# A decoder layer on one core: a call of weight sums in another stage, a pair of loads behind another load, one cast in place of two

## The chip, the core and the metric

The kernel runs on one core of a Trainium2 chip. The core has TensorE (PE) for matmuls, VectorE (DVE) and ScalarE (ACT) for elementwise work, GpSimd (POOL) and SyncE (SP). The engines work side by side and meet at semaphores; each takes its own instructions in order. Loads and stores are issued by an engine's instruction stream and are carried out by 16 DMA engines. In this kernel SyncE issues nearly all loads and GpSimd all stores. The metric is the time of one execution in microseconds; the median of several is compared.

## The reference

One layer: a token mixer (a gated short convolution beside a multi-scale causal pooling, then an output projection) and an MLP with squared ReLU, each modulated by a conditioning vector and closed by a residual and a LayerNorm. Tokens 2048, width 1024, hidden width 4096, all in fp32.

```python
mod = (silu(c) @ w_ada + b_ada)[:, None, :]
sh1, sc1, g1, sh2, sc2, g2 = jnp.split(mod, 6, axis=-1)

h = x * (1.0 + sc1) + sh1
z = h @ w_in                                   # 1024 -> 2048
gate_b, gate_c, v_conv, v_pool = jnp.split(z, [512, 1024, 1536], axis=-1)
y_conv = gate_b * _short_conv(gate_c * v_conv, conv_w)
y_pool = _multiscale_pool(v_pool, w_pool, pool_scale)
mix = jnp.concatenate([y_conv, y_pool], axis=-1) @ w_out
x = _layer_norm(ALPHA * x + (1.0 + g1) * mix, ln1_g, ln1_b)

h = x * (1.0 + sc2) + sh2
f = jnp.square(jax.nn.relu(h @ w_mlp_in)) @ w_mlp_out   # 1024 -> 4096 -> 1024
x = _layer_norm(ALPHA * x + (1.0 + g2) * f, ln2_g, ln2_b)
```

## The kernel before

**Tokens and stages.** The 2048 tokens are worked on in two blocks of 1024 (b = 0 and 1). Each block goes through an input projection, the mixing, an output projection (`out_proj`), the up projection of the MLP in eight groups of 512 hidden columns (`up`, g = 0 to 7) and the down projection in 14 steps (`down`, n = 0 to 13).

**One fp32 product is three matmuls.** `split` (L82 to L85) makes of a tile its rounded part (a cast on ScalarE, L84, the "hi" or high part) and the remainder (a subtract on VectorE, L85, the "lo" or low part). `mm3` (L88 to L91) then issues high by high (L89), high by low (L90) and low by high (L91), all into one PSUM bank.

**Seven products for eight.** The large matrix products are done in 2 x 2 blocks with seven block products, which need sums of blocks. Sums of weight blocks are made on the chip and kept in DRAM: `sum_block` loads four blocks of 128 x 512 on SyncE (L961), does four additions or subtractions on VectorE (L96, by `tt`) and issues four stores on GpSimd (L968). It is a generator: its first part issues the loads, its second does the rest. `quarter_sums` takes the next of twelve such pieces of work from a list (source `in_w2q`, goal `wquart`); the results are read in the down projection of the second block alone. `quarter_sums_after` does one whole call in tiles of pool c. Calls stand, before the change, at steps 2, 3, 4, 5, 6, 7 and 10 of the first block's down projection, at two places of the second block's input projection, and in groups 1, 3 and 5 of the second block's up projection (through `aside`, in tiles of pool o).

**Buffers.** Tiles of 128 x 1024 fp32 come from pools with a fixed number of buffers: h 28 (split parts), o 10, c 2, w 6 and r 5 (loaded blocks), and 8 PSUM banks. A load into a buffer waits until the last reader of what stood in it has ended, or until a store from it has landed. Since SyncE issues in order, a load that waits holds all the loads behind it.

**The down projection of the first block.** For step n, `down_operands` loads four blocks of the activations (`usum`, pool r) and four of the weights (`in_w`, pool w), and each is split. The operands of step n + 1 are set up in the code ahead of step n's matmuls; a scheduler then places each instruction into its engine's order. Step n's product is drained from PSUM by `keep` (a copy on ScalarE, L1256) or `add` (VectorE). In steps 5 to 8 `residual` also loads two tiles each of the first sub-layer's result (`nsave`, L1151, pool r), scales them by two broadcast rows (`ag` and `ab`) on VectorE and stores them (`rsave`, L1154).

**The up projection of the second block.** `up(g)` does the seven products in the order 0, 1, 2, 3, 4, 5, 6 and joins and squares the results on VectorE and ScalarE; `save` stores them. The weights of group g + 1 are four blocks, a11 to a22, in pool r, loaded ahead while group g runs. Beside them runs `aside`: in groups 1, 3 and 5 a call of weight sums; for groups 2, 4 and 6 two row broadcasts (L221, 512 KB each, from `in_rows`) and a pair of `nsave` tiles (L1020) into pool o, whose load is started a group early by `next(extra[1])` and whose sums are done in the group itself.

**The output projection of the second block.** `out_proj` walks through seven steps with `matmuls`; after the last matmul of each quarter t a function drains the bank on VectorE (`begin`, `end`, L896 among them). `ops.whole(n)` loads the operands of step n; `whole(6)` has the last of them.

**The opening.** `first_group` begins the input projection of the first block. Its weights come in eight k-blocks; for k = 0 the weight half is cast on ScalarE in two pieces of 128 x 256 (L377 and L386), and each has its remainder on VectorE. The matmuls of k = 0 are 24 at L418, those of k = 1 to 7 are 168.

Of the kernel before, what the change touches and what calls it, by code (L numbers as in the profile page):

```python
# [8 lines left out]
F32 = mybir.dt.float32  # L9
F32R = mybir.dt.float32r  # L10
AF = mybir.ActivationFunctionType
ALU = mybir.AluOpType
# [5 lines left out]
H = 512  # L18
# [11 lines left out]
Q = H // 2  # L30
# [13 lines left out]
def tile_hybrid_layer(ctx: ExitStack, tc: tile.TileContext, opening, xT, x, wada, vec, win0, win,  # L44
                      wins, wpool, wout, wmix, w1, w2, w2q, rows, out):
    nc = tc.nc
# [18 lines left out]
    def t_o(w=T, dt=F32):  # L65
        return mk(big, [P, w], dt, "o", 10)
# [28 lines left out]
    def tt(out_, a, b_, op):  # L95
        done = nc.vector.tensor_tensor(out_, a, b_, op=op)  # L96
        recent[0] = done.ins
        return done
# [258 lines left out]
    def first_group(A):  # L357
        ps = {}

        def loads(k):  # L360
            rows_ = [t_h(F32) for _ in range(2)]
            wr, a = t_r(), t_o()
            for i, r in enumerate(rows_):
                in_turn(r, wada[2 * k + i])
            in_turn(wr[:, :H], win0[k])
            in_turn(a, xT[0, k])
            return rows_, wr, [a[:, hs] for hs in halves]

        done = ada_first()
        wr, a = w0, [w0[:, H:], x0[:, H:]]  # L370
        for k in range(KD):
            wt = t_w()
            hi, lo = t_h(), t_h()
            A.append((hi, lo))
            opened.append(done.ins)
            if k == 0:
                nc.scalar.copy(wt[:, :Q], wr[:, :Q])  # L377
            with tc.issue_after(done.ins):
                if k:
                    nc.scalar.copy(wt[:, :H], wr[:, :H])  # L380
                    tt(wt[:, H:], wr[:, :H], wt[:, :H].bitcast(F32), ALU.subtract)
                for x_, hs in zip(a, halves):
                    high = shifted(hi, x_, k, hs)
                    if k == 0 and hs.start == 0:
                        with tc.issue_after(high.ins):
                            high = nc.scalar.copy(wt[:, Q:H], wr[:, Q:H])  # L386
                        for c in (0, Q):
                            tt(wt[:, H + c : H + c + Q], wr[:, c : c + Q], wt[:, c : c + Q].bitcast(F32), ALU.subtract)
                    if k:
                        nc.scalar.activation(x_, x_, AF.Identity, bias=mod[:, 2 * k + SH1 : 2 * k + SH1 + 1],  # L390
                                             scale=mod[:, 2 * k + SC1 : 2 * k + SC1 + 1])
            if k + 1 < KD:
                rows_, wr_n, a_n = loads(k + 1)
            if k == 0:
                with tc.issue_after(high.ins):
                    for hs, bank in zip(halves, cond_banks):
                        nc.scalar.copy(cond[:, hs], bank)
            elif k + 1 < KD:
                done = dot(2 * k + 2, rows_[0])
            with tc.issue_after(done.ins):  # L400
                for x_, hs in zip(a, halves):
                    if k == 0:
                        sc, sh = (mod[:, 2 * k + i : 2 * k + i + 1] for i in (SC1, SH1))
                        nc.vector.tensor_scalar(x_, x_, sc, sh, op0=ALU.mult, op1=ALU.add)
                    low = tt(lo[:, hs], x_, hi[:, hs].bitcast(F32), ALU.subtract)
            if k + 1 < KD:
                with tc.issue_after(low.ins):
                    for i in range(k > 0, 2):
                        dot(2 * k + 2 + i, rows_[i])
                done = biased(2 * k + 2, 2 * k + 4)  # L410
                wr, a = wr_n, a_n
            for h, hs in enumerate(halves):
                for p in range(3):
                    for m in range(4):
                        if k == 0 and p == 0:
                            ps[m, h] = t_ps()
                        w = (H if p == 1 else 0) + m * P
                        nc.tensor.matmul(ps[m, h], wt[:, w : w + P], A[k][p // 2][:, hs],  # L418
                                         start=k == 0 and p == 0, stop=k == KD - 1 and p == 2)
        return ps  # L420
# [396 lines left out]
    class Operands:  # L817
# [18 lines left out]
        def weights(self, n, g, tile=None):  # L836
            w = ORDER[self.steps[n]][1]
            r = tile or t_r()
            nc.sync.dma_start(r, wosum[g, int(w) - 1] if len(w) == 1 else
                              gout[int(w[1]) - 1, 2 * int(w[0]) - 2 + g])  # L840
            self.w[n, g] = parts(r)


# [19 lines left out]
    def out_proj(b, ops):  # L863
        R, X, Y = [], {}, {}
# [10 lines left out]
        def matmuls(n, banks, new, ks, then):  # L875
            for t in range(4):
                if new and ks[0] == 0:
                    banks[t] = t_ps()
                for k in ks:
                    g, p = k // 2, k % 2  # L880
                    (uh, ul), (wh, wl) = ops.a[n, g], ops.w[n, g]
                    cs = slice(p * H + t * P, p * H + t * P + P)
                    mm3(banks[t], uh[:, cs], ul[:, cs], wh[:, halves[p]], wl[:, halves[p]],
                        new and k == 0, k == 3, not new)
                if then:
                    then(t, banks[t])
# [5 lines left out]
        def end(t, cs, other, scalar=1.0):  # L892
            if t not in mv:
                mv[t] = mk(sm, [P, 8], F32, "mv", 8)
            i = 4 + cs.start // H
            begun[:] = [nc.vector.scalar_tensor_tensor(R[t][:, cs], R[t][:, cs], scalar, other, op0=ALU.mult,  # L896
                                                       op1=ALU.add, accum_out=mv[t][:, i : i + 1]).ins]

        def scale():
            t = late.pop()  # L900
            begun[:] = [nc.vector.tensor_scalar(R[t], R[t], mv[t][:, 0:1], mv[t][:, 6:7], op0=ALU.add,
                                                op1=ALU.mult).ins]
            nc.gpsimd.dma_start(nsave[t], R[t])
# [42 lines left out]
        if b == 0:  # L946
            sum_weights(w1[0], w1sum[0], lambda w: t_w(F32), begun[0], halves[1 : 2])
        ops.whole(6)
        scale()
        matmuls(5, X, False, every, lambda t, ps: end(t + 4, hi_, ps))  # L950
        back(0)
        matmuls(6, X, False, every, last_row)
        scale()
# [3 lines left out]
    def sum_block(src, dst, tiles, p):  # L957
        a, b_ = tiles(T), tiles(T)
        b22, b12, b11, b21 = a[:, :H], a[:, H:], b_[:, :H], b_[:, H:]
        for i, r in ((3, b22), (1, b12), (0, b11), (2, b21)):  # L960
            nc.sync.dma_start(r, src[i][:, p])  # L961
        yield
        tt(b22, b22, b12, ALU.subtract)
        tt(b12, b12, b11, ALU.subtract)
        tt(b11, b22, b11, ALU.add)
        tt(b21, b21, b11, ALU.subtract)
        for i, r in ((2, b22), (0, b12), (1, b11), (3, b21)):
            nc.gpsimd.dma_start(dst[i][:, p], r)  # L968
# [37 lines left out]
    def quarter_sums_after(after):  # L1006
        sums = quarter_sums(t_c)
        next(sums)
        with tc.issue_after(after):
            next(sums, None)  # L1010

    def sum_out(g, tiles):
        sum_blocks([gout[i % 2, i // 2 * 2 + g] for i in range(4)], wosum[g], tiles)
# [1 line left out]
    def aside(g):  # L1015
        if g in REST:
            ag, ab = row(t_o(D), rows[0]), row(t_o(D), rows[1])
            tiles = [t_o(D) for _ in REST[g]]
            for t, r in zip(REST[g], tiles):
                nc.sync.dma_start(r, nsave[t])  # L1020
            yield
            for t, r in zip(REST[g], tiles):
                rest_of(t, r, ag, ab)
        elif g in QUARTER_SUMS:
            sums = quarter_sums(t_o)
            next(sums)
            if g in (3, 5):
                early = t_o()
                nc.sync.dma_start(early, usum[g // 2 - 1, 0])
            yield  # L1030
            next(sums, None)
            if g in (3, 5):
                save_quarters(early, QUARTERED[0], g // 2 - 1)

    def up(g, B, fine):
# [21 lines left out]
        def save(r, i):  # L1057
            if fine and i in QUARTERED and (i or g > 1):
                save_quarters(r, QUARTERED[i], g)
            else:  # L1060
                nc.gpsimd.dma_start(usum[g, i], r)
# [27 lines left out]
        product(4, X, False)  # L1089
        join(c22, X)  # L1090
        save(c22, 3)
        if extra and g:
            next(extra[1], None)
        if g == 0:
            yield
# [12 lines left out]
            nc.scalar.activation(c21[:, ps[p]], X[p], AF.Relu)  # L1108
        nc.scalar.activation(c21, c21, AF.Square)
        save(c21, 1)  # L1110
        s7 = t_o()
        tt(s7, c21, c11, ALU.subtract)
        save(s7, 7)
# [45 lines left out]
    def down(b, F, g2, close):  # L1159
        X, Y = {}, {}  # L1160
# [170 lines left out]
        for n, (i, hf) in enumerate(steps):  # L1331
# [4 lines left out]
                ready = operands(n + 1)  # L1336
            if b == 0 and n < 2:
                ada(G2 + 4 * n, G2 + 4 * n + 4, nc.sync.dma_start, lambda: t_o(D))
            if b == 0 and n in (2, 3, 4, 5, 6, 7, 10):
                quarter_sums_after(ready[1][1])  # L1340
            if b == 0 and 2 <= n < 6:
                sum_x(n - 2, ready[1])
# [235 lines left out]
```

## Time and profile before

| | |
|---|---|
| time, median of 3 runs | 1744.46 us (1742.77 to 1746.51) |
| the profiled execution | 1744.09 us |
| its span | 1742.3 us |
| mean granted clock of TensorE in it | 0.997 |
| instructions in it | 22974 |
| moved by DMA in it | 503.59 MB, mean 289 GB/s |

The span runs from the first to the last instruction recorded; 1.8 us of the execution lie around it. The profile cuts the span into 40 equal slices of 43.6 us. Each digit is the busy share of an engine in tenths, PEclk the granted clock of TensorE in tenths of full speed, DMA the busy share of the DMA engines:

```profile
PE   9999999999999999989999999998999999999998
...
DVE  8897898787777876769786789696877767998897
ACT  5323367554544653536573344774454555776451
POOL 0222220122322001100000100103322221000020
PEclk9999999999999999999999999999999999999999
DMA  9988877678888999998773366557787579998671
```

Of the places named below, the time 753 us (the first block's down projection) lies in the 18th slice, 1100 us (the second block's output projection) in the 26th, and 1214 us (its up projection) in the 28th. In the chain of waits, "issue" is time in which an engine waited for nothing that the profile shows. In a timeline a row is the start, the length, the engine, the line and the operation, and in brackets the idle time ahead of it with what ended it.

### The profile page before, as it was taken

How to read it: one execution, taken by the hardware profiler on the slowest of the kernel's cores; microseconds unless marked ns; L12 is line 12 of the kernel's file. 1: busy time of each engine (PE TensorE's matmuls, PEld its weight loads, DVE VectorE, ACT ScalarE, POOL GpSimd, SP SyncE). 2: the span in 40 equal slices, each digit the busy share in tenths (PEclk: the TensorE clock that was granted, in tenths of full speed). 3: DMA queues.
4: the chain of work that ended last, by engine and by line, in shares of the span. 5: the costliest groups of instructions: out<-in, count | busy, mean ns of one | idle time of the engine just before them, and what ended most of it. 6: DMA issues, size and time to landing. Idle time of an engine off the chain costs nothing.

```text
span 1742.3 us, 22974 instructions
## 1 busy us (share of the span) xinstructions
PE 1720.8 (99%) x8142; PEld 1445.8 (83%) x8142; DVE 1389.7 (80%) x1841; ACT 890.8 (51%) x1207; POOL 271.3 (16%) x483
## 2 busy tenths in 40 slices
PE   9999999999999999989999999998999999999998
PEld 7888888788888888878888888887888888999886
DVE  8897898787777876769786789696877767998897
ACT  5323367554544653536573344774454555776451
POOL 0222220122322001100000100103322221000020
PEclk9999999999999999999999999999999999999999
DMA  9988877678888999998773366557787579998671
GB/s 385 345 313 336 322 274 254 253 274 329 322 326 328 384 403 381 384 340 329 280 265 122 141 223 215 206 192 290 264 314 273 216 250 380 418 365 315 237 259 55
DMA packets 157427, 503.59 MB, mean 289 GB/s; under 512 B 18800, under 2 KB 19584, under 8 KB 157312
## 3 DMA queue, kind: packets, MB, share of 16 engines
q1 hardware_dynamic: 107712, 328.56, 51.8%
q0 software_dynamic: 49600, 173.58, 26.0%
q8 instruction: 63, 1.03, 0.2%
q14 instruction: 52, 0.43, 0.1%
HBM read 344.24 MB, written 157.82 MB: 288 GB/s over the span
## 4 chain that ended last, share of the span: by engine, by line
PE 85%; issue 5%; DMA 5%; DVE 3%; POOL 1%; ACT 0%; SPq 0%; DVEq 0%; POOLq 0%; ACTq 0%
PE ps L89 25%; PE ps L91 25%; PE ps L90 25%; PE ps L1195 7%; PE ps L418 2%; DMA o<-hsave 1%; DVE o L96 1%; DMA usum<-o 1%; PE ps L770 1%; DMA r<-in_w 1%; DVE w L85 1%; DMA o<-in_w2q 0%; DVE h L85 0%; DMA wquart<-c 0%; DMA r<-usum 0%
## 5 line engine op out<-in xcount | busy, mean ns | idle before, releaser
L91 PE MATMUL ps<-h,w 128*128 128x512 f32 x1312 | 510.7, 390 | 4.8 <-DVE w L85 4.8
L89 PE MATMUL ps<-h,w 128*128 128x512 f32 x1312 | 511.0, 390 | 1.3 <-DVE o L96 1.1
L90 PE MATMUL ps<-h,w 128*128 128x512 f32 x1312 | 510.7, 390 | 0.0
L89 PE MATMUL ps<-h,h 128*128 128x512 f32 (+1 forms) x936 | 363.3, 388 | 4.7 <-ACT o L1256 4.7
L91 PE MATMUL ps<-h,h 128*128 128x512 f32 (+1 forms) x936 | 363.4, 388 | 0.0
L90 PE MATMUL ps<-h,h 128*128 128x512 f32 (+1 forms) x936 | 363.1, 388 | 0.0
L84 ACT CAST h<-r 128x1024 fp32r<-128x1024 f32 (+1 forms) x202 | 205.6, 1022 | 258.8 <-PE ps L90 70.9
L85 DVE TENSOR_TENSOR h<-r,h 128x1024 fp32r<-128x1024 f32 (+1 forms) x202 | 238.3, 1184 | 82.9 <-ACT h L84 82.5
L84 ACT CAST w<-r 128x1024 fp32r<-128x1024 f32 x156 | 164.2, 1054 | 256.5 <-PE ps L90 247.5
L91 PEld LDWEIGHTS ps<-h,w 128*128 128x128 f32 x1312 | 246.6, 188 | 56.6 <-DVE w L85 5.2
L89 PEld LDWEIGHTS ps<-h,w 128*128 128x128 f32 x1312 | 246.6, 188 | 53.7 <-DVE o L96 1.1
L90 PEld LDWEIGHTS ps<-h,w 128*128 128x128 f32 x1312 | 246.7, 188 | 51.3 <-DVE h L85 0.3
L85 DVE TENSOR_TENSOR w<-r,w 128x1024 fp32r<-128x1024 f32 x156 | 190.3, 1220 | 81.8 <-ACT w L84 81.1
L89 PEld LDWEIGHTS ps<-h,h 128*128 128x128 f32 x936 | 176.2, 188 | 41.2 <-ACT o L1256 5.1
L91 PEld LDWEIGHTS ps<-h,h 128*128 128x128 f32 x936 | 176.2, 188 | 36.0
L90 PEld LDWEIGHTS ps<-h,h 128*128 128x128 f32 x936 | 176.1, 188 | 35.8
L85 DVE TENSOR_TENSOR h<-w,h 128x1024 fp32r<-128x1024 f32 x130 | 159.4, 1226 | 9.4 <-ACT h L84 9.1
L84 ACT CAST h<-w 128x1024 fp32r<-128x1024 f32 x130 | 136.5, 1050 | 22.5 <-DMA w<-in_w 15.4
L96 DVE TENSOR_TENSOR o<-o,o 128x512 f32<-128x512 f32 (+2 forms) x172 | 127.9, 747 | 6.7 <-DMA o<-hsave 4.5
L96 DVE TENSOR_TENSOR o<-o,ps 128x512 f32<-128x512 f32 (+1 forms) x150 | 96.0, 650 | 42.3 <-PE ps L91 39.7
L1195 PEld LDWEIGHTS ps<-h,h 128*128 128x128 f32 x1008 | 121.1, 192 | 0.1
L1195 PE MATMUL ps<-h,h 128*128 128x256 f32 x1008 | 121.1, 283 | 0.0
(175 smaller groups left out, 1532.7 us busy)
## 6 DMA issues: line engine op xcount, KB each, us to landing
r<-usum SPq DMA_DIRECT2D x88, 512.0 KB, 6.6
usum<-o POOLq DMA_DIRECT2D x64, 512.0 KB, 5.3
w<-w2sum SPq DMA_DIRECT2D x64, 512.0 KB, 6.1
r<-in_w SPq DMA_DIRECT2D x60, 512.0 KB, 6.2
r<-uquart SPq DMA_DIRECT2D x42, 512.0 KB, 5.9
o<-in_w SPq DMA_DIRECT2D x72, 256.0 KB, 6.0
w2sum<-o POOLq DMA_DIRECT2D x64, 256.0 KB, 7.4
usum<-c POOLq DMA_DIRECT2D x26, 512.0 KB, 5.8
```

The lines of the kernel that those rows point to most:

```text
L84: high = nc.scalar.copy(hi, src)
L85: return high.ins, nc.vector.tensor_tensor(lo, src, hi.bitcast(F32), op=ALU.subtract).ins
L89: nc.tensor.matmul(ps, whi, xhi, start=first, stop=False, skip_group_check=goes_on)
L90: nc.tensor.matmul(ps, whi, xlo, start=False, stop=False, skip_group_check=goes_on)
L91: nc.tensor.matmul(ps, wlo, xhi, start=False, stop=last, skip_group_check=goes_on)
L96: done = nc.vector.tensor_tensor(out_, a, b_, op=op)
L418: nc.tensor.matmul(ps[m, h], wt[:, w : w + P], A[k][p // 2][:, hs], start=k == 0 and p == 0, stop=k == KD - 1 and p == 2)
L770: nc.tensor.transpose(ps[:, t * P : t * P + P], R[4 * h + t][:, k * P : k * P + P], ident)
L1195: nc.tensor.matmul(ps, a[:, us], w[:, gs], start=not begun, stop=hf == 1 and g == 3 and a is ul, skip_group_check=True)
```

## The change

Three edits. (1) The call of weight sums at step n = 7 of the first block's down projection is dropped, and one call is put into the second block's output projection: its loads are issued behind the last weight load of `ops.whole(6)`, and its sums come in two pieces behind quarters 2 and 3 of `matmuls(5, ...)`. For that `sum_block` has a second `yield`. The twelve pieces are the same; those behind the dropped call each come one call earlier or in the new place. (2) In `up(1)` the loads of the third group's rows and pair (`aside(2)`) are started behind the last `save` but one, and no longer behind `save(c22, 3)`. (3) In `first_group` the cast for k = 0 is one of 128 x 512, and so is its remainder.

```diff
@@ first_group
             if k == 0:
-                nc.scalar.copy(wt[:, :Q], wr[:, :Q])
+                nc.scalar.copy(wt[:, :H], wr[:, :H])
             with tc.issue_after(done.ins):
                 if k:
                     nc.scalar.copy(wt[:, :H], wr[:, :H])
-                    tt(wt[:, H:], wr[:, :H], wt[:, :H].bitcast(F32), ALU.subtract)
+                tt(wt[:, H:], wr[:, :H], wt[:, :H].bitcast(F32), ALU.subtract)
                 for x_, hs in zip(a, halves):
                     high = shifted(hi, x_, k, hs)
-                    if k == 0 and hs.start == 0:
-                        with tc.issue_after(high.ins):
-                            high = nc.scalar.copy(wt[:, Q:H], wr[:, Q:H])
-                        for c in (0, Q):
-                            tt(wt[:, H + c : H + c + Q], wr[:, c : c + Q], wt[:, c : c + Q].bitcast(F32), ALU.subtract)
@@ Operands.weights
-            nc.sync.dma_start(r, wosum[g, int(w) - 1] if len(w) == 1 else
-                              gout[int(w[1]) - 1, 2 * int(w[0]) - 2 + g])
+            self.loaded = nc.sync.dma_start(r, wosum[g, int(w) - 1] if len(w) == 1 else
+                                            gout[int(w[1]) - 1, 2 * int(w[0]) - 2 + g]).ins
@@ out_proj
         ops.whole(6)
+        if b:
+            sums = quarter_sums(t_c)
+            with tc.issue_after(ops.loaded):
+                next(sums)
         scale()
-        matmuls(5, X, False, every, lambda t, ps: end(t + 4, hi_, ps))
+
+        def last_half(t, ps):
+            end(t + 4, hi_, ps)
+            if b and t > 1:
+                with tc.issue_after(begun[0]):
+                    next(sums, None)
+
+        matmuls(5, X, False, every, last_half)
@@ sum_block
         tt(b12, b12, b11, ALU.subtract)
+        yield
         tt(b11, b22, b11, ALU.add)
@@ quarter_sums_after
         with tc.issue_after(after):
-            next(sums, None)
+            for _ in sums:
+                pass
@@ aside
-            next(sums, None)
+            for _ in sums:
+                pass
@@ up
         save(c22, 3)
-        if extra and g:
+        if extra and g > 1:
             next(extra[1], None)
...
         save(c21, 1)
+        if extra and g == 1:
+            next(extra[1])
@@ down
-            if b == 0 and n in (2, 3, 4, 5, 6, 7, 10):
+            if b == 0 and n in (2, 3, 4, 5, 6, 10):
                 quarter_sums_after(ready[1][1])
```

How instructions move is best seen at two places. A row is the line in the code, the operation, and the tiles it writes and reads with the number that the tile has in its kernel; the numbers differ between the two kernels, since tiles are counted through. In the code after, L961 becomes L967, L1121 becomes L1132, L1123 becomes L1134, L1151 becomes L1162, L514 becomes L509 and L1020 becomes L1028.

**The first block's down projection, around step 7.** SyncE's order before, from the last load for step 7 on; r tiles from `nsave` are the pair for `residual`, c tiles are those of the call of sums:

```order
L1123 DMA w_976_6143<-in_w2 128x1024
L961 DMA c_981_6153<-in_w2q 128x512 x2
L1151 DMA r_983_6167<-nsave_151 128x1024
L961 DMA c_982_6154<-in_w2q 128x512 x2
L1151 DMA r_984_6172<-nsave_151 128x1024
L1121 DMA r_985_6277<-usum_149 128x1024
L1123 DMA w_986_6279<-in_w2 128x1024
L1121 DMA r_991_6289<-usum_149 128x1024
```

SyncE's order after, from the same load on:

```order
L1134 DMA w_976_6141<-in_w2 128x1024
L1162 DMA r_981_6151<-nsave_151 128x1024
L1162 DMA r_982_6156<-nsave_151 128x1024
L1134 DMA w_984_6263<-in_w2 128x1024
L1132 DMA r_983_6261<-usum_149 128x1024
L1134 DMA w_990_6275<-in_w2 128x1024
L1134 DMA w_996_6287<-in_w2 128x1024
L1132 DMA r_989_6273<-usum_149 128x1024
```

The c loads are gone from between the nsave loads, and weight loads now stand ahead of the usum load that has the second place in its step (r_991 before, r_989 after). In both, that usum load takes the buffer of r_969, and the first nsave load that of r_957; the second nsave load waits for the store of r_952 to `rsave`.

VectorE's order at the same place before, from the last operation on step 7's first operands on:

```order
L85 TENSOR_TENSOR h_968_6126<-w_964_6119,h_967_6125 128x1024
L96 TENSOR_TENSOR r_983_6167<-r_983_6167,o_921_5817 128x1024
L96 TENSOR_TENSOR r_983_6167<-r_983_6167,o_922_5819 128x1024
L85 TENSOR_TENSOR h_972_6134<-r_969_6129,h_971_6133 128x1024
L85 TENSOR_TENSOR h_974_6138<-w_970_6131,h_973_6137 128x1024
L96 TENSOR_TENSOR r_984_6172<-r_984_6172,o_921_5817 128x1024
L96 TENSOR_TENSOR r_984_6172<-r_984_6172,o_922_5819 128x1024
L85 TENSOR_TENSOR h_978_6146<-r_975_6141,h_977_6145 128x1024
```

VectorE's order after, from the same operation on:

```order
L85 TENSOR_TENSOR h_968_6124<-w_964_6117,h_967_6123 128x1024
L96 TENSOR_TENSOR r_981_6151<-r_981_6151,o_921_5815 128x1024
L96 TENSOR_TENSOR r_982_6156<-r_982_6156,o_921_5815 128x1024
L96 TENSOR_TENSOR r_981_6151<-r_981_6151,o_922_5817 128x1024
L85 TENSOR_TENSOR h_972_6132<-r_969_6127,h_971_6131 128x1024
L85 TENSOR_TENSOR h_974_6136<-w_970_6129,h_973_6135 128x1024
L96 TENSOR_TENSOR r_982_6156<-r_982_6156,o_922_5817 128x1024
L85 TENSOR_TENSOR h_978_6144<-r_975_6139,h_977_6143 128x1024
```

The multiplication of the second nsave tile (r_984 before, r_982 after) moved from behind the low part of r_969 to ahead of it.

**The second block's up projection, group 1.** SyncE's order before, from the third weight block of group 2 on; o_1568 and o_1569 belong to the call of sums, the next four tiles to `aside(2)`, r_1591 is the fourth weight block:

```order
L514 DMA r_1590_9896<-in_w1 128x1024
L961 DMA o_1568_9744<-in_w2q 128x512 x2
L961 DMA o_1569_9745<-in_w2q 128x512 x2
L221 DMA o_1573_9793<-in_rows 128x1024
L221 DMA o_1574_9795<-in_rows 128x1024
L1020 DMA o_1575_9797<-nsave_151 128x1024
L1020 DMA o_1576_9798<-nsave_151 128x1024
L514 DMA r_1591_9897<-in_w1 128x1024
```

SyncE's order after, from the same block on:

```order
L509 DMA r_1590_9894<-in_w1 128x1024
L967 DMA o_1568_9742<-in_w2q 128x512 x2
L967 DMA o_1569_9743<-in_w2q 128x512 x2
L509 DMA r_1591_9895<-in_w1 128x1024
L221 DMA o_1582_9874<-in_rows 128x1024
L221 DMA o_1583_9876<-in_rows 128x1024
L1028 DMA o_1584_9878<-nsave_151 128x1024
L1028 DMA o_1585_9879<-nsave_151 128x1024
```

The fourth weight block moved from behind the four loads of `aside(2)` to ahead of them.

VectorE's order there before, from the second of the weight sums on; r_1602 is the sum of two weight blocks, ps tiles are banks of the group's products, o_1567 is what `join` adds them to, and w_1593 and w_1598 are low parts for products 0 and 1 of group 2:

```order
L96 TENSOR_TENSOR o_1568_9744<-o_1568_9744,o_1569_9745 128x512
L96 TENSOR_TENSOR o_1567_9741<-o_1567_9741,ps_1500_9354 128x512
L96 TENSOR_TENSOR o_1569_9745<-o_1568_9744,o_1569_9745 128x512
L96 TENSOR_TENSOR o_1569_9745<-o_1569_9745 128x512
L96 TENSOR_TENSOR o_1567_9741<-o_1567_9741,ps_1501_9367 128x512
L85 TENSOR_TENSOR w_1593_9903<-r_1588_9894,w_1592_9902 128x1024
L96 TENSOR_TENSOR o_1561_9706<-o_1561_9706,ps_1565_9715 128x512
L96 TENSOR_TENSOR r_1602_9977<-r_1590_9896,r_1591_9897 128x1024
L96 TENSOR_TENSOR o_1561_9706<-o_1561_9706,ps_1566_9728 128x512
L85 TENSOR_TENSOR w_1598_9936<-r_1589_9895,w_1597_9935 128x1024
```

VectorE's order there after, from the same sum on:

```order
L96 TENSOR_TENSOR o_1568_9742<-o_1568_9742,o_1569_9743 128x512
L96 TENSOR_TENSOR o_1567_9739<-o_1567_9739,ps_1500_9352 128x512
L96 TENSOR_TENSOR o_1569_9743<-o_1568_9742,o_1569_9743 128x512
L96 TENSOR_TENSOR r_1602_9975<-r_1590_9894,r_1591_9895 128x1024
L96 TENSOR_TENSOR o_1569_9743<-o_1569_9743 128x512
L96 TENSOR_TENSOR o_1567_9739<-o_1567_9739,ps_1501_9365 128x512
L85 TENSOR_TENSOR w_1593_9901<-r_1588_9892,w_1592_9900 128x1024
L96 TENSOR_TENSOR r_1590_9894<-r_1588_9892,r_1590_9894 128x1024
L96 TENSOR_TENSOR o_1561_9704<-o_1561_9704,ps_1565_9713 128x512
L96 TENSOR_TENSOR r_1588_9892<-r_1602_9975,r_1588_9892 128x1024
L96 TENSOR_TENSOR o_1561_9704<-o_1561_9704,ps_1566_9726 128x512
L85 TENSOR_TENSOR w_1598_9934<-r_1589_9893,w_1597_9933 128x1024
```

The sum r_1602, which reads the fourth weight block, moved ahead of the add on ps_1501 and of the low part w_1593.

## The prediction

> **What bounds the kernel now.** I read the busy table first, then what TensorE waited for.
>
> ```profile
> PE 1720.8 (99%) x8142; PEld 1445.8 (83%) x8142; DVE 1389.7 (80%) x1841; ACT 890.8 (51%) x1207; POOL 271.3 (16%) x483
> ```
>
> ```profile
> PE ps L91 <- DVE w L85: 4.8, 1, 4.8
> PE ps L89 <- ACT o L1256: 4.7, 1, 4.7
> PE ps L418 <- ACT h L229: 1.2, 2, 0.9
> PE ps L89 <- DVE o L96: 1.1, 2, 0.7
> ```
>
> TensorE is busy for 99% of the span, so work taken from another engine gains nothing by itself: only TensorE's gaps can be won. Two single waits, 4.8 and 4.7 us, are far above the rest. The timeline of TensorE shows where they stand; the rows of 1213.83 and 14.75 are for later.
>
> ```profile
> 14.75 38.39 PE L418 MATMUL ps<-h,w 128*128 128x512 f32 x168 [0.30 <-ACT h L229]
> ...
> 753.17 0.39 PE L91 MATMUL ps<-h,h 128*128 128x512 f32 x1
> 758.22 0.50 PE L89 MATMUL ps<-h,h 128*128 128x512 f32 x1 [4.67 <-ACT o L1256]
> ...
> 1213.83 0.50 PE L89 MATMUL ps<-h,w 128*128 128x512 f32 x1 [0.19 <-ACT c L1045]
> 1214.17 0.40 PE L90 MATMUL ps<-h,w 128*128 128x512 f32 x1
> 1219.34 0.77 PE L91 MATMUL ps<-h,w 128*128 128x512 f32 x1 [4.78 <-DVE w L85]
> ```
>
> Matmuls start 38.39 / 168 = 0.2285 us apart. **Stall B** lies in the first block's down projection and loses 758.22 − 753.17 − 0.23 = 4.82. **Stall C** lies in up group 2 of the second block and loses 1219.34 − 1214.17 − 0.23 = 4.94. Behind each, the table by windows (length, then sum and count for PE, PEld, DVE, ACT and POOL, then the granted clock, the DMA share, GB/s) has a stretch at half clock:
>
> ```profile
> 758.60:762.02 3.42, 3.42 (x10) 2.65 (x9) 2.80 (x3) 3.02 (x5) 1.08 (x2) 0.50 0.99 405
> 1219.40:1222.82 3.42, 3.42 (x8) 2.72 (x9) 3.42 (x5) 0.00 (x0) 0.75 (x1) 0.50 1.03 246
> ```
>
> Each loses another 0.5 × 3.42 = 1.71. So B costs 6.53 and C 6.65; I found no half clock behind the smaller gaps.
>
> **Stall C: the load moved ahead of the row pair.** SyncE's queue issues in order. Before, the fourth weight block of group 2 (r_1591) stands behind two row broadcasts and the nsave pair. The rows: SyncE, the landing of the first row broadcast, the chain of waits, VectorE.
>
> ```profile
> 1183.95 3.58 SPq L221 DMA_DIRECT2D o<-in_rows  x2
> ```
>
> ```profile
> DMA to landing us min/median/max: 11.8/12.0/12.1
> ```
>
> ```profile
> 1191.42 13.35 DMA r<-in_w
> ```
>
> ```profile
> 1183.06 1.22 DVE L85 TENSOR_TENSOR w<-r,w 128x1024 fp32r<-128x1024 f32 x1
> ...
> 1193.68 0.68 DVE L96 TENSOR_TENSOR o<-o,ps 128x512 f32<-128x512 f32 x1
> ...
> 1204.86 1.22 DVE L96 TENSOR_TENSOR r<-r,r 128x1024 f32<-128x1024 f32 x1 [8.76 <-DMA r<-in_w]
> ...
> 1218.07 1.22 DVE L85 TENSOR_TENSOR w<-r,w 128x1024 fp32r<-128x1024 f32 x1
> ```
>
> The block is issued at 1191.42, lands 13.35 later at 1204.77, and VectorE stands 8.76 us at its first use; everything behind it is late, down to the low part at 1218.07 for which TensorE waits in product 2. After, only the four weight-sum loads precede it. Its buffer is free when the subtract of 1183.06 ends (1184.28), so it is issued where the first row broadcast was, and by that row's 11.8 it lands at 1184.0 + 11.8 = 1195.8, nine microseconds earlier.
>
> What is late next? VectorE's order changes too: the sum that needs r_1591 now stands ahead of the add that ran at 1193.68, and that add frees a PSUM bank. Work: sum 1.14 (spacing of such 1.22 us rows), two half-width operations of 0.60: the bank is free at 1195.8 + 2.4 = 1198.2. Products take 24 × 0.2285 = 5.48 us; counted back from product 2 at 1213.83 less the 0.35 lost just before it, product 1 begins at 1208.0, product 0 at 1202.5, product 6 of the group before at 1197.1, and its second half, which takes that bank, at 1199.8. Margin 1.6. From 1198.2 VectorE has nine full-width and two half-width operations up to the low part for product 2: 9 × 1.14 + 2 × 0.60 = 11.5, done at 1209.7 against a need at 1213.5. Margin 3.8. So all of C goes: **−6.65**. What is unknown is the landing: the quick end is 6 us or so (gain the same), the late end the 13.35 of the old row, which gives 1197.7 and a loss of 0.1 us. I take 11.8, the load that stood at this very place. The pair and its rows now land later; their first use on VectorE stands behind the low part for product 2 in its order.
>
> **Stall B: a call of weight sums is taken out.** The chain, SyncE, VectorE, ScalarE in that order:
>
> ```profile
> 736.06 6.82 DMA wquart<-c
> ...
> 750.58 5.96 DMA r<-usum
> ```
>
> ```profile
> 740.76 0.82 SPq L961 DMA_DIRECT2D c<-in_w2q  x2
> 741.68 0.38 SPq L1151 DMA_DIRECT2D r<-nsave  x1
> ```
>
> ```profile
> 733.95 1.22 DVE L85 TENSOR_TENSOR h<-r,h 128x1024 fp32r<-128x1024 f32 x1
> ...
> 746.92 2.48 DVE L96 TENSOR_TENSOR r<-r,o 128x1024 f32<-128x1024 f32 x2 [7.76 <-DMA r<-nsave]
> 749.33 1.22 DVE L85 TENSOR_TENSOR h<-r,h 128x1024 fp32r<-128x1024 f32 x1
> ```
>
> ```profile
> 756.64 1.04 ACT L84 CAST h<-r 128x1024 fp32r<-128x1024 f32 x1 [3.06 <-DMA r<-usum]
> 757.59 0.58 ACT L1256 COPY o<-ps 128x512 f32<-128x512 f32 x1
> ```
>
> The removed call's loads (740.76) waited for buffers whose stores were still under way, and held SyncE; behind them the nsave load (741.68) came late; VectorE waited for it until 746.92, did two operations on it and the low part of 749.33, which frees the buffer of the usum load issued at 750.58. That lands at 756.54; ScalarE casts it, and only then makes the copy of 757.59 that frees TensorE's bank: TensorE goes on 1.68 after the landing.
>
> After, those c loads are gone, but VectorE's order changes with them: both nsave tiles are multiplied ahead of that low part. The second (r_982) needs the buffer that a store has to leave, of which GpSimd's timeline and the tile's landing say:
>
> ```profile
> 733.72 0.54 POOL L1154 DMA_DIRECT2D rsave<-r  x1 [0.59 <-DVE r L96]
> ```
>
> ```profile
> DMA to landing us min/median/max: 7.9/7.9/7.9
> ```
>
> ```profile
> DMA to landing us min/median/max: 5.1/5.1/5.1
> ```
>
> The first nsave load can go when the subtract of 733.95 ends (735.2, instead of 741.68). The second cannot go before 733.72 + 7.9 = 741.6; I take 742.3, as the first load now shares the DMA engines with that store. The nsave row took 5.1 with two c loads beside it (0.52 MB, 1.3 us at the 405 GB/s above); without them 3.9, so it lands at 746.2 instead of 746.8. Three operations later, as before (746.8 to 750.58 is 3.78), the usum load is issued at 750.0; by its old 5.96 it lands at 755.9, and 1.68 later, at 757.6, TensorE goes on. Loss 757.6 − 753.17 − 0.23 = 4.2 instead of 4.82. The head-of-line wait is thus **moved to another store, not removed**. The half clock: both stretches are 3.42 long and begin 0.38 and 0.06 after the restart, as if periods of 3.42 were judged and one with no more than 0.38 of work were called idle. An idle time of 4.0 holds such a period in (4.0 + 0.38 − 3.42) / 3.42 = 28% of positions, so I leave the half clock out. B falls from 6.53 to 4.2: **−2.3**. Bounds: if the second load did not bind (landed by 744), loss 2.0; if the usum load also took 4 us, nothing; on the other side the shared store lands a whole 1.3 us later and the loss with half clock is 7.2, 0.7 more than before.
>
> The Trainium skill, "TensorE: Matmul & The Clock Gate", section "Part 1: The HAM clock gate", gives a free-running window of 3413 ns and half rate after one idle window. The two rows of 3.42 agree; by it alone, with no work allowed in the window, a gap of 4.0 would lose the clock in 17% of positions.
>
> A rule of the skill speaks against this part: "DMA: Bandwidth & Descriptors", section "Queues, rings and completion order", says that a DMA engine takes turns between queues, packet by packet. So a load issued earlier on SyncE's queue slows a store on GpSimd's; by it the gating store would land up to the 1.3 us later, and B would be the 7.2 of the bound. That is part of the first rival.
>
> **The call moved into the output projection.** Four loads, four sums of 0.68 us, four stores. VectorE and GpSimd there:
>
> ```profile
> 1105.60 0.69 DVE L896 SCALAR_TENSOR_TENSOR o<-o,ps 128x512 f32<-128x512 f32 x1 [1.18 <-PE ps L91]
> ...
> 1108.33 0.69 DVE L896 SCALAR_TENSOR_TENSOR o<-o,ps 128x512 f32<-128x512 f32 x1 [2.04 <-PE ps L91]
> ```
>
> ```profile
> 1110.51 0.53 POOL L782 DMA_DIRECT2D hsave<-r  x1 [5.86 <-ACT r L775]
> ```
>
> The loads stand behind the last weights of the projection, over 20 us ahead of the sums. A pair of sums (1.3) fits into the idle 2.04 ahead of 1108.33 and the next pair behind it, and GpSimd is idle for 5.86. I cost it at **0**; the bounds are nothing and 4 × 0.60 = 2.4, if every sum stood on TensorE's path.
>
> **The opening cast.** ScalarE and VectorE:
>
> ```profile
> 7.53 0.41 ACT L377 CAST w<-r 128x256 fp32r<-128x256 f32 x1 [4.86 <-DMA r<-in_opening]
> ...
> 11.72 0.62 ACT L380 CAST w<-r 128x512 fp32r<-128x512 f32 x1 [1.11 <-DMA r<-in_win]
> ```
>
> ```profile
> 11.27 1.22 DVE L207 SCALAR_TENSOR_TENSOR h<-h,o 128x1024 f32<-128x1024 f32 x1
> ```
>
> The first cast becomes 0.21 longer (0.62 against 0.41), and the first matmuls start later by it. But TensorE waits 0.30 at 14.75 for a tile of the second block, which hangs on VectorE's operation of 11.27. VectorE does one subtract of 0.61 in place of two of 0.33 and then the same tiles, and I get 11.28 for that operation. The 0.21 goes out of the later 0.30: **0**, between −0.1 and +0.2.
>
> **The sum** on the profiled run's own 1744.09 (span 1742.3 and 1.8 around it): 1744.09 − 6.65 − 2.3 = 1735.1. The median shown is 1744.46, 0.37 above that run: **1735.5**.
>
> **The rivals.** *B stays whole*: the wait moves to the store and the load behind it, TensorE resumes near 758 and loses the clock. For it: VectorE's new order and the 7.9 of the store. 1744.46 − 6.65 = 1737.8. *Both go*: the second nsave load is quick and the usum load lands by 751.7. Against it: it would take 4 us off a chain of which I can name 0.6. 1744.46 − 6.65 − 6.53 = 1731.3. *The bank in product 6*: r_1591 lands 2.4 past the 1197.4 from which the margin is gone: 1737.9. *C only changes its place*: it lands between 1201.5 and 1204, product 6 stands for 4 to 7 us and half clock follows: 1741 to 1746. *The other side*: the load gains nothing by its new place and lands at 1204.8 as before. Then product 6 stands for 7.4 and loses 1.71 of clock, 9.1 in place of 6.65, and with B whole the kernel is **slower**: 1744.46 + 2.45 = 1746.9. It is worse than before from a landing of 1202.7 on. Against both: the row broadcast at that place landed at 1195.8.
>
> **How the numbers follow.** Forecast 0.50, B whole 0.24, both gone 0.11, product 6 late 0.05, C only moved 0.06, the other side 0.04. The range takes in the first four, with the runs' spread at its ends (1.7 below their median, 2.05 above): 1731.3 − 1.7 = 1729.6 to 1737.9 + 2.0 = 1739.9. A measurement can tell about 0.2% (3.5 us) from no change. Faster by more: the first four, 0.90. Within it: C only moved and half of the other side, 0.08. Slower: the other half, 0.02.
>
> **What would show it.** For C: the in_w load that VectorE's first sum needs is issued near 1184 and lands near 1196, and the wait on the L85 low part with its half clock is gone; a wait of L89 on VectorE's add in product 6 would show the late bank. For B: an nsave load at about 735, one behind the rsave store at about 742, VectorE waiting until about 746, and a TensorE gap near 4 us with full clock behind it. Wrong would be: a gap at the output projection's sums, a longer span up to 53 us, or a gap of 5 us and more at either place.

## The result and the profile after

The changed kernel takes 1736.48 us (median of 6 runs, 1735.78 to 1738.29), against 1745.10 for the kernel before (6 runs, 1742.76 to 1746.51) beside it: a ratio of **0.9955, 95% interval 0.9942 to 0.9967**, faster by 0.45%. The forecast was 1735.5, range 1729.6 to 1739.9. The profiled run of the changed kernel took 1735.78, its span is 1734.0.

What TensorE waited for, in the kernel after (in all, times, longest):

```profile
PE ps L89 <- ACT o L1267: 5.6, 1, 5.6
PE ps L127 <- DVE tmp L122: 1.1, 1, 1.1
PE ps L413 <- ACT h L229: 0.6, 1, 0.6
```

The wait of 4.8 on the low part (stall C) is gone. The wait on the copy (L1267, L1256 before; stall B) is not: 5.6 instead of 4.7. TensorE's timeline after, at the places where the same matmul was shown before:

```profile
752.06 0.39 PE L91 MATMUL ps<-h,h 128*128 128x512 f32 x1
758.02 0.80 PE L89 MATMUL ps<-h,h 128*128 128x512 f32 x1 [5.57 <-ACT o L1267]
...
761.55 0.39 PE L89 MATMUL ps<-h,h 128*128 128x512 f32 x1
...
1212.99 0.39 PE L89 MATMUL ps<-h,w 128*128 128x512 f32 x1
...
1215.26 0.39 PE L90 MATMUL ps<-h,w 128*128 128x512 f32 x1
...
1725.85 0.28 PE L91 MATMUL ps<-h,h 128*128 128x256 f32 x1
```

Its counterparts before that have not been shown yet:

```profile
345.11 0.50 PE L89 MATMUL ps<-h,w 128*128 128x512 f32 x1 [0.67 <-DVE o L96]
...
761.93 0.43 PE L89 MATMUL ps<-h,h 128*128 128x512 f32 x1
...
1222.87 0.39 PE L90 MATMUL ps<-h,w 128*128 128x512 f32 x1
...
1733.49 0.28 PE L91 MATMUL ps<-h,h 128*128 128x256 f32 x1
```

The same matmul in both, after less before, tells where the 8.3 us between the spans were won and lost:

| up to | before | after | difference | won (−) or lost (+) on the way |
|---|---|---|---|---|
| the last matmul ahead of stall B | 753.17 | 752.06 | −1.11 | −1.11 |
| behind B and its half clock | 761.93 | 761.55 | −0.38 | +0.73 |
| the start of product 2 of group 2 | 1213.83 | 1212.99 | −0.84 | −0.46 |
| behind C and its half clock | 1222.87 | 1215.26 | −7.61 | −6.77 |
| the last matmul | 1733.49 | 1725.85 | −7.64 | −0.03 |
| the end of the span | 1742.3 | 1734.0 | −8.3 | −0.66 |

C gave 6.77 and, with the small wait ahead of it, 7.23. B gave nothing and took 0.73 in this pair of profiles. The 1.11 ahead of B are not the change's: small gaps like the one at 345.11, in a stretch where no instruction was changed, are there in one profile and missing in the next. In the ten profiles of this case, all with the same work and order there, gaps above 0.8 us between the starts of two matmuls came four times near 317 and once near 345. The 0.66 at the end lie behind the last matmul.

**Stall C went as worked out.** SyncE and VectorE after:

```profile
1183.73 0.33 SPq L509 DMA_DIRECT2D r<-in_w  x1
```

```profile
1194.62 1.22 DVE L96 TENSOR_TENSOR r<-r,r 128x1024 f32<-128x1024 f32 x1 [2.07 <-DMA r<-in_w]
...
1196.37 0.68 DVE L96 TENSOR_TENSOR o<-o,ps 128x512 f32<-128x512 f32 x1
...
1207.62 1.22 DVE L85 TENSOR_TENSOR w<-r,w 128x1024 fp32r<-128x1024 f32 x1
```

The load is issued at 1183.73 and VectorE uses it at 1194.62 (forecast 1184 and 1195.8). The bank that the new order put at risk is free at 1196.37 + 0.68 = 1197.05 (forecast 1198.2), 2.2 ahead of its need (1212.99 − 2.5 × 5.48 = 1199.3). The low part for product 2 is done at 1208.84 (forecast 1209.7), before the product begins at 1212.99.

**Stall B only moved.** The chain of waits after, from the store on:

```profile
732.94 8.95 DMA rsave<-r
...
741.91 3.74 DMA r<-nsave
...
748.02 1.23 DVE h L85
...
749.27 7.08 DMA r<-usum
...
757.39 0.59 ACT o L1267
```

SyncE's timeline has the two nsave loads as one row from 734.41 to 742.23:

```profile
734.41 7.82 SPq L1162 DMA_DIRECT2D r<-nsave  x2
```

The second of them is issued 0.02 after the rsave store lands (732.94 + 8.95 = 741.89). Before, the chain ran over a wquart store (736.06 + 6.82 = 742.88). VectorE stands for the nsave loads as before, and ScalarE stands at the cast ahead of the copy:

```profile
742.36 1.23 DVE L96 TENSOR_TENSOR r<-r,o 128x1024 f32<-128x1024 f32 x1 [3.96 <-DMA r<-nsave]
745.74 2.36 DVE L96 TENSOR_TENSOR r<-r,o 128x1024 f32<-128x1024 f32 x2 [2.16 <-DMA r<-nsave]
748.02 1.22 DVE L85 TENSOR_TENSOR h<-r,h 128x1024 fp32r<-128x1024 f32 x1
```

```profile
756.44 1.04 ACT L84 CAST h<-r 128x1024 fp32r<-128x1024 f32 x1 [6.24 <-DMA r<-usum]
757.39 0.58 ACT L1267 COPY o<-ps 128x512 f32<-128x512 f32 x1
```

The theory after this, not yet shown here: B is an order, and twice so. On VectorE a multiplication that waits for an nsave load stands ahead of the low part that frees a loading buffer; on ScalarE copies that are ready stand behind a cast that waits for the load into that buffer. The rival is the number of bytes: the DMA engines are 99% busy from 752 to 766 before and 96% after, and if that is a limit, no order helps.

### The profile page after: what moved, and what is told of

The parts are those of the page before. It is cut to its first block, busy times and chain, and to the rows that moved or that the text cites. A ratio compares the mean times of both kernels' runs of the same rounds, so it can differ in the third digit from the quotient of the medians.

```text
span 1734.0 us, 22976 instructions
## 1 busy us (share of the span) xinstructions
PE 1718.8 (99%) x8142; PEld 1446.1 (83%) x8142; DVE 1388.4 (80%) x1840; ACT 890.8 (51%) x1206; POOL 272.1 (16%) x483
## 3 DMA queue, kind: packets, MB, share of 16 engines
q8 instruction: 63, 1.03, 0.2%
## 4 chain that ended last, share of the span: by engine, by line
PE 94%; issue 3%; DMA 1%; DVE 1%; POOL 0%; ACT 0%; SPq 0%; DVEq 0%; POOLq 0%; ACTq 0%
PE ps L89 28%; PE ps L90 28%; PE ps L91 28%; PE ps L1206 7%; PE ps L413 3%; PE ps L765 1%; DMA rsave<-r 1%; DMA r<-usum 0%; DMA r<-in_opening 0%; DMA r<-nsave 0%; POOL wquart L975 0%; DVE o L96 0%; DVE h L85 0%; POOL rsave L1165 0%; POOL xsum L593 0%
```

## The experiments

All times are medians; each ratio is to runs of the kernel before on the same chip (1744.49 for the first four, 1744.11 for the other four).

### The load of group 2's fourth weight block alone (`e_pair`)

The kernel before with this edit:

```diff
         save(c22, 3)
-        if extra and g:
+        if extra and g > 1:
             next(extra[1], None)
...
         save(c21, 1)
+        if extra and g == 1:
+            next(extra[1])
```

> Before with the second edit alone (the fourth weight block of group 2 ahead of the rows and the pair). Theory: stall C hangs on the place of that load alone. The load is issued near 1184 to 1185 and lands near 1196, the gap at product 2 and its half clock are gone, the gap of about 5 us in the first block's down projection stays: 6.7 to 7.3 us faster, about 1738. Rival: C went because of what the other edits moved in time; then a gap of 2 us or more stays in group 2 and the gain is under 4.

1738.70 (6 runs), ratio 0.9969 (0.9957 to 0.9981), which is 5.4 us faster (3.3 to 7.5); the expected 6.7 to 7.3 lie in the interval, above its middle. The only wait of TensorE that is listed from 20 us on:

```profile
PE ps L89 <- ACT o L1258: 5.8, 1, 5.8
```

The other large wait is gone. The gap in the first block's down projection stands. The edit alone takes C away, and the rival falls.

### The call of weight sums alone (`e_call`)

The kernel before with the edits to `Operands.weights`, `out_proj`, `sum_block`, `quarter_sums_after`, `aside` and the list of steps in `down`, as in the diff of the change.

> Before with the first edit alone (one call of weight sums taken from step 7 of the first block's down projection and put into the second block's output projection). Theory: the wait only moves, to the rsave store and the nsave load behind it, and TensorE goes on between 757 and 759 as it did before: no change, within 1.5 us of before, gap of 4 to 6 us at step 8 with half clock, nothing above 0.3 us at the output projection. Rival (the forecast): the stall is about 2.3 shorter and so is the time.

1745.39 (12 runs), ratio 1.0004 (0.9995 to 1.0013). TensorE's waits:

```profile
PE ps L89 <- ACT o L1270: 5.4, 1, 5.4
PE ps L91 <- DVE w L85: 4.8, 1, 4.8
```

No gain shows: the interval leaves at most 0.9 us. The 2.3 of the forecast are ruled out. No gap shows at the output projection. The theory holds: TensorE goes on at 758.59.

### The opening cast alone (`e_open`)

The kernel before with the edit to `first_group`.

> Before with the third edit alone (the opening cast whole). Theory: from the start of the first cast to VectorE's first L207 operation 3.74 us as in both profiles, so no change of the time beyond 0.3 us; the 0.70 by which k = 1 began later in the changed kernel came from the landing of the opening load. Rival: the whole cast itself costs 0.7 us.

1744.35 (12 runs), ratio 1.0000 (0.9992 to 1.0009): nothing, within 1.6 us. That the changed kernel's k = 1 began 0.7 later has its cause in the opening load. ScalarE's first cast in the kernel of `e_pair`, which has not this edit, and in that of `e_copy`, which has it:

```profile
8.29 0.41 ACT L377 CAST w<-r 128x256 fp32r<-128x256 f32 x1 [5.46 <-DMA r<-in_opening]
```

```profile
7.60 0.62 ACT L377 CAST w<-r 128x512 fp32r<-128x512 f32 x1 [4.72 <-DMA r<-in_opening]
```

The late landing came without the edit, the early one with it. From the first cast to VectorE's L207 operation it is 11.27 − 7.53 = 3.74 before and 12.02 − 8.27 = 3.75 after. The wait at B, in a kernel that has the call at step 7 as before, is longer here than the 4.7 of the first profile:

```profile
PE ps L89 <- ACT o L1251: 5.4, 1, 5.4
```

### ScalarE's copies ahead of the casts (`e_copy`)

The changed kernel with:

```diff
         def keep(t, cs, ps):
-            nc.scalar.copy(F[t][:, cs], ps)
+            kept[:] = [nc.scalar.copy(F[t][:, cs], ps).ins]
...
             elif n + 1 < len(steps):
-                ready = operands(n + 1)
+                with tc.issue_after(kept[0]) if b == 0 and n == 8 else nullcontext():
+                    ready = operands(n + 1)
```

> The changed kernel, with ScalarE's casts for step 9 of the first block's down projection ordered behind the four copies that drain step 7. Theory: stall B is an order on ScalarE, copies that are ready standing behind a cast that waits for a load; the load itself is not needed for 20 us. TensorE then has no gap above 1 us at step 8 and no half clock there, and the time is 6 to 7.5 us below the changed kernel, about 1729.5. Rival: the stretch is bound by what the DMA engines can move, so the operands are late anyway and a gap of 3 us or more comes back in steps 8 to 10; time within 3 us of the changed kernel.

1736.20 (6 runs), ratio 0.9955 (0.9942 to 0.9968): no gain over the changed kernel that these intervals, some 2 us to each side, could show. The gap at step 8 is gone; at step 9 TensorE now waits four times, 4.2 us in all:

```profile
777.01 0.50 PE L90 MATMUL ps<-h,h 128*128 128x512 f32 x1 [2.38 <-DVE h L85]
779.28 0.50 PE L90 MATMUL ps<-h,h 128*128 128x512 f32 x1 [0.61 <-DVE h L85]
```

That is the gap which the rival had asked for, but its reason is not there. VectorE, GpSimd and the table by windows:

```profile
764.08 2.48 DVE L96 TENSOR_TENSOR r<-r,o 128x1024 f32<-128x1024 f32 x2 [10.03 <-DMA r<-nsave]
773.46 1.23 DVE L96 TENSOR_TENSOR r<-r,o 128x1024 f32<-128x1024 f32 x1 [6.89 <-DMA r<-nsave]
774.61 1.22 DVE L85 TENSOR_TENSOR h<-r,h 128x1024 fp32r<-128x1024 f32 x1
```

```profile
766.87 0.53 POOL L1165 DMA_DIRECT2D rsave<-r  x1 [14.25 <-DVE r L96]
```

```profile
770.00:777.00 7.00, 4.63 (x21) 3.50 (x19) 3.54 (x4) 0.00 (x0) 0.00 (x0) 1.00 0.28 81
```

The DMA engines are 28% busy while TensorE waits. VectorE stands twice at operations on nsave tiles, for 10.0 and 6.9 us; the second nsave load, issued at 770.12, had to wait for the rsave store of 766.87, which took 3.2. Only behind it come the low parts of step 9, 1.14 us apart; TensorE's waits are two of them apart (779.28 − 777.01 = 2.27). So ScalarE's order was the last link of stall B. That VectorE's pair is the root, which then made the next gap, is a reading of these rows; the next experiment tests it. The theory was right on step 8 and wrong in expecting the time.

### VectorE's pair behind the low parts (`e_rest`)

The changed kernel with:

```diff
-            tt(r, r, ag, ALU.mult)
-            tt(r, r, ab, ALU.add)
+            with tc.issue_after(after[1]):
+                tt(r, r, ag, ALU.mult)
+                tt(r, r, ab, ALU.add)
             nc.gpsimd.dma_start(rsave[t], r)
             if t % 2:
-                yield
+                after = yield
```

> The changed kernel, with VectorE's four operations on each pair of nsave tiles ordered behind the last low part of the step whose operands were set up just before; ScalarE's order is left to itself. Theory: the root of stall B and of the gap at step 9 in the kernel with the copies first is VectorE standing at a multiplication whose nsave load waits for an rsave store. With it behind the low parts the buffer of the gating usum load is free near 739, that load is issued near 743 (SyncE still waits for the store) and lands near 749, before TensorE needs the copy at 752: no gap above 1 us in steps 8 to 10, 6 to 7 us below the changed kernel, about 1730. Rival: SyncE's own wait at the nsave load and the bytes in this stretch hold the usum load anyway: a gap of 3 us or more stays.

1731.95 (6 runs), ratio 0.9921 (0.9908 to 0.9934): by the two ratios 0.34% or 5.9 us below the changed kernel, where 6 to 7 were expected. The wait of 5.57 has become one of 0.90, and one of 0.3 behind it, with no half clock:

```profile
754.48 0.50 PE L89 MATMUL ps<-h,h 128*128 128x512 f32 x1 [0.90 <-ACT o L1268]
```

ScalarE still has the casts of two operand pairs of step 9 ahead of the copies, and they wait for loads, if much shorter. The theory holds, but for this last 1 us. One thing the edit does not separate: it orders VectorE alone, but the loads on SyncE have moved too. A usum load now stands ahead of both nsave loads, the first of which was issued at 734.41 in the changed kernel:

```profile
741.00 0.33 SPq L1132 DMA_DIRECT2D r<-usum  x1
741.42 0.95 SPq L1162 DMA_DIRECT2D r<-nsave  x2
```

So what is shown is the effect of the new order on both engines; how much of it is VectorE's alone is not.

### Both orders (`e_both`)

The edits of `e_copy` and `e_rest` together.

> The changed kernel with both orders: VectorE's pair behind the low parts, and ScalarE's casts for step 9 behind the copies of step 7. Theory: no gap above 1 us in steps 8 to 10, and since one of the two orders is enough at step 8, within 1 us of the kernel with VectorE's order alone, about 1730. Rival: the DMA engines bound the stretch, gaps of 2 us or more come back in steps 9 to 11.

1729.19 (4 runs), ratio **0.9908 (0.9894 to 0.9922)**: by the two ratios 0.47% or 8 us below the changed kernel, in which B costs 7.2 (758.02 − 752.06 − 0.23 = 5.73, and some 1.5 at half clock). No gap is left in the down projection. VectorE's low part of 746.52 now comes ahead of the pair, and ScalarE copies as soon as TensorE lets it:

```profile
746.52 1.23 DVE L85 TENSOR_TENSOR h<-r,h 128x1024 fp32r<-128x1024 f32 x1 [5.16 <-ACT h L84]
747.66 1.22 DVE L85 TENSOR_TENSOR h<-w,h 128x1024 fp32r<-128x1024 f32 x1
748.80 3.49 DVE L96 TENSOR_TENSOR r<-r,o 128x1024 f32<-128x1024 f32 x3
```

```profile
748.65 0.59 ACT L1269 COPY o<-ps 128x512 f32<-128x512 f32 x1 [1.21 <-PE ps L91]
```

It is 2.8 below `e_rest` by the medians where the theory had said within 1; the two intervals overlap, so how much the second order adds to the first stays open.

### Both orders, and the call back at step 7 (`e_both_call7`)

As `e_both`, with:

```diff
-        if b:
-            sums = quarter_sums(t_c)
-            with tc.issue_after(ops.loaded):
-                next(sums)
         scale()
...
-            if b and t > 1:
-                with tc.issue_after(begun[0]):
-                    next(sums, None)
...
-            if b == 0 and n in (2, 3, 4, 5, 6, 10):
+            if b == 0 and n in (2, 3, 4, 5, 6, 7, 10):
```

> As the kernel with both orders, but the call of weight sums stands at step 7 of the first block's down projection again and none in the output projection. Theory: the stall was an order, not the call's bytes or its place, so with the orders right the call costs nothing there: within 1.5 us of the kernel with both orders. Rival: the call's loads and stores (1 MB each way) are what is too much for the stretch: 2 us or more slower, with a gap in steps 8 to 10.

1729.05 (4 runs), ratio 0.9906 (0.9892 to 0.9920): the same as with the call in the output projection. The table by windows of this kernel, and of the changed one:

```profile
742.00:749.00 7.00, 7.00 (x33) 5.79 (x32) 4.69 (x6) 2.59 (x3) 0.54 (x1) 1.00 1.02 379
749.00:756.00 7.00, 7.00 (x32) 5.80 (x31) 6.93 (x9) 5.05 (x7) 2.70 (x5) 1.00 1.03 405
```

```profile
742.00:749.00 7.00, 7.00 (x33) 5.79 (x32) 4.48 (x4) 0.80 (x1) 0.54 (x1) 1.00 0.86 324
749.00:756.00 7.00, 3.45 (x16) 2.52 (x14) 7.00 (x7) 1.20 (x2) 0.54 (x1) 1.00 0.98 297
```

With the call and without a stall the engines moved 379 and 405 GB/s in the 14 us where the changed kernel moved 324 and 297 and stalled, though they were busy for 0.86 and 0.98 of the time there. The bytes fit; the rival falls. Where the call stands makes no difference that can be measured, in either direction.

### The pair of step 7 put off by a step (`e_step9`)

The changed kernel with:

```diff
-            if b == 0 and base <= n < base + 4:
+            if b == 0 and n in (base, base + 1, base + 3, base + 4):
```

> The changed kernel with the nsave pairs in steps 5, 6, 8 and 9 in place of 5 to 8, no order forced. Theory: nothing waits for an rsave store ahead of the low parts set up in step 7, so the gap at step 8 is below 1.5 us; as VectorE's order then has a multiplication by a row ahead of low parts one step later, part of it comes back in steps 9 to 11: 2 to 6 us below the changed kernel. Rival: the stall at step 8 stays above 4 us because the operands' loads are late for want of bandwidth.

1735.56 (4 runs), ratio 0.9943 (0.9926 to 0.9961). The pair of step 8 moves with it, to step 9. The gap at step 8 is gone, which says once more that the nsave pair of step 7 made it. But TensorE waits later, in step 11, and goes on at half clock (0.50 from 821.79 to 825.20):

```profile
821.79 0.80 PE L90 MATMUL ps<-h,h 128*128 128x512 f32 x1 [3.36 <-DVE h L85]
```

The chain back from there was not taken apart; VectorE is busy ahead of it with the closing LayerNorm of the first rows. Where the time came back is shown, why at that place is not. The expected 2 to 6 us were at most found at their lower end (2.1 by the two ratios).

## Why the prediction was right, and where it was wrong

- **Stall C, −6.65:** right, in mechanism and size. It measured 6.77, and 7.23 with the 0.46 just ahead of product 2 which the sum had left out. Every step came within 1.2 us of its number, each on the early side. `e_pair` shows that this edit alone does it. The rivals "the bank in product 6", "C only changes its place" and "the other side" did not happen: the margin was 2.2. One figure beside the sum was off: a landing at 1197.7 would have cost 0.3, not 0.1, by the prediction's own 1197.4, from which the margin is gone.
- **Stall B, −2.3:** wrong; it came out at **+0.73**, and `e_call` shows the edit to be worth nothing (interval −0.9 to +2.3 us). The first rival, that the stall stays whole, happened, and so did one of the prediction's own signs of being wrong, a gap of 5 us and more. The path was in the prediction: the wait moved from the wquart store to the rsave store and the nsave load behind it. The sizes on it failed. From the issue of that store to TensorE's restart the sum has 757.6 − 733.72 = 23.9 us, the profile after 758.02 − 732.94 = 25.1:
  - Up to the issue of the second nsave load it was 9.0 (741.91 − 732.94), not 8.6 (742.3 − 733.72). The store took 9.0 us here and in `e_call` and 8.8 in `e_copy`, all with the early nsave load beside it, but 7.9, 8.5 and 8.4 in the kernel before, `e_pair` and `e_open`. That agrees with the 0.7 added for sharing; the 7.9 under it was the shortest of three.
  - From there to the issue of the usum load it was 7.4 (749.27 − 741.91), not 7.7 (750.0 − 742.3).
  - The usum load took 7.08, not 5.96, the largest error. It took 5.3 to 7.1 us in the six profiles of kernels that force no order on VectorE and have the pairs in steps 5 to 8, so 5.96 was one draw of a spread.
  - TensorE came to the stall 19.1 us behind the store's issue (752.06 − 732.94), not 19.5 (753.17 − 733.72), and so stood longer by that as well.

  The loss to start from was a draw too. TensorE waited 4.7, 5.8 and 5.4 us at this place in the kernel before, `e_pair` and `e_open`, all with the call at step 7, and 5.6 and 5.4 in the changed kernel and `e_call`, without it. The 0.6 by which the gap was to shrink and the +0.73 that was measured both lie inside that spread.
- **The half clock, left out at a chance of 28%:** wrong with the gap. Of the −2.3 it is the larger part, 1.71. The idle time was 5.57 rather than 4.0, for which the prediction's own rule gives (5.57 + 0.38 − 3.42) / 3.42 = 74%. The half clock ended within 3.1 us of the restart at 758.02, against 3.8 before, as it had begun while TensorE still stood (granted clock 0.93 from 755 to 758).
- **The call in the output projection, 0:** right; no gap there, and the same time in `e_both` and `e_both_call7`. VectorE took the sums in the idle time around the drain.
- **The opening, 0:** right; ratio 1.0000 in `e_open`.
- **The total:** 1735.1 was forecast for the profiled run and 1735.78 measured. The near agreement owes something to luck: B missed by 3.0 us, while C's extra 0.6, the gaps near 317 and 345 and the end of the span gave 2.3 or so back, and the last two are no part of the change.

## What to carry to other kernels

Here a queue waited for a store, and taking out the work that waited uncovered the next wait of the same sort. Before counting such a gain, follow the new order to the next instruction that stands at the head of an engine and depends on a store and a load. The better handle here was the order: work that must wait for a round trip behind the work that frees a buffer, and a copy that drains PSUM ahead of casts whose loads are still on the way. Count a stall from the event that starts the chain behind it, here the issue of a store, and take the lengths on that chain from several profiles: a gain of 0.6 us cannot be read off one profile when a single load on the way takes 5.3 to 7.1.

## What the runs showed of the hardware that was not expected

A DMA share near 1 did not mean that no more could be moved. In the table by windows the same share of 0.98 to 1.03 stands beside 297 GB/s in one kernel and 405 in another for the same 7 us of the program. And the landing of the very first weight load varied by 0.7 us between profiles of kernels that do the same up to it (first casts at 7.53, 7.60, 8.27 and 8.29), which is enough to pass for the effect of a small edit at that place. TensorE's clock fell to half behind an idle time of 3.36 us (`e_step9`, granted clock 0.50 from 821.79 to 825.20) and stayed whole behind one of 2.38 us (`e_copy`, 1.00 from 777 to 784).
